# Neighbourhood attention scores: plain float32 matmuls on 64x64 tiles of the array in place of split operands on the whole array

## The chip, the core and the metric

The kernel runs on one core of a Trainium2 chip. A core has five engines with a queue each, which work side by side and wait for one another through semaphores: PE (TensorE, matrix multiplication; PEld is its weight load), DVE (VectorE), ACT (ScalarE), POOL (GpSimd) and SP (SyncE, which here issues nearly all DMA transfers). PE reads SBUF and writes PSUM, which has eight banks of 128 partitions x 2 KB. The metric is the device time of one execution in microseconds.

## The reference

One layer of a bidirectional encoder over 1024 tokens of width 1024, all in float32: a token mixer, a cross-attention into 256 memory tokens and a gated feed-forward part, each with a residual and a layer norm. The mixer has a recurrent group (mLSTM) and a neighbourhood-attention group of 8 heads x 64, whose outputs go side by side through one output projection. Only the second group matters here. The 1024 tokens are a grid of 16 rows x 64 columns, and each query sees a window of 8 rows x 16 columns, clipped at the borders, with a learned bias by relative place:

```python
s = jnp.einsum('bhrqd,bhrkd->bhrqk', qg, k_rows) * (NA_DIM ** -0.5)
...
s = jnp.where(mask, s + bias, -jnp.inf)
p = jax.nn.softmax(s, axis=-1)
o = jnp.einsum('bhrqk,bhrkd->bhrqd', p, v_rows)
```

## The kernel before

The program runs as a chain of stages. The stage of this change stands between the recurrent group and the output projection of the mixer. `nqk_d` in DRAM holds the transposed queries and keys, `nv_d` the values; an earlier stage wrote them.

**Blocks.** The stage loops over four pairs of heads `p` and four column blocks `cb`. A block is 16 of the 64 grid columns; the keys that it can see lie in 32 columns from `CB[cb]` on. Its 16 grid rows are four groups `g` of 4 rows x 16 columns, 64 queries; groups 0 and 3 see 8 rows of keys (256 keys of the 32 columns), groups 1 and 2 see 12 rows (384). Partitions 0 to 63 of a query or key tile belong to the first head of the pair, 64 to 127 to the second.

**One group.** A score tile `S` in PSUM has the 64 queries of the first head in its partitions 0 to 63, those of the second in 64 to 127, and the keys along the free dimension. `mm3` (L223 to L226) makes it with three matmuls over the whole 128x128 array: each operand is split into a rounded part (`h`) and a remainder (`l`) in the type float32r, and the products h·h, h·l and l·h are summed. So that one matmul serves both heads, the query tile is block-diagonal: 64x64 of one head, 64x64 of the other, zeros elsewhere, set once by memsets (L1131, L1132). ACT makes `qsh` (L1189, two copies per block) and `kh` (L1193), POOL the remainders `qsl` (L1190) and `kl` (L1194), in the first block DVE. Then DVE adds the bias table `tb` and takes the minimum (L1209, shown as a custom operation), ACT takes the exponential and its sum (L1211), DVE inverts and scales (L1213, L1214), PE transposes in pieces of 128 keys (L1219, into `tp`), ACT copies to `PT` (L1220). The value matmuls `o` (L1145, `pv_gen`) of a block follow during the next block: plain float32, one per head and piece, each on 64 columns of the array, so that the two heads use its two column halves. ACT and DVE split the result into `X2h` and `X2l` (L229, L230).

**Tables.** `tb` is mask minus bias, three tables per column type (groups 1 and 2 share one), built by POOL (L1181) from `wide`, one DMA per pair. There are three column types, and column blocks 1 and 2 share one.

**Work beside it.** `out_a` is the first half of the output projection, over the recurrent group's output: `fill` matmuls (L224 to L226, 128x512, twelve per half of a 128-token tile) into the one bank of tag Z. DVE adds the residual (L1089), which frees the bank; POOL adds the bias `bmo` (L1094); SP stores the tile to `part` (L1096) and loads the next residual `r` from `h` (L1072). The second half, `out`, over this stage's output, follows and partly overlaps the last pair. `mix` (L30) interleaves `na_gen` with `out_a` by the costs that they yield.

**Order.** The tile framework puts each engine's instructions into one fixed order, which a timeline model of its own sets at build time; each engine then works strictly in that order. Tags and buffer counts say which tiles share memory: a score bank comes from tag Y (three banks), the value bank from X (two). A load into memory that an earlier stage used waits for that stage. Tiles of the pool `vecs` (`vec0` to `vec2`) exist through the whole program, those of `nw` only from this stage on. In the same stretch the framework has also placed small work of the next stage: the load of the cross-attention bias `b_xo` into `vec2` (L114) and its scaling on DVE (L1453).

## Time and profile before

| | us |
|---|---|
| three timed runs, median (lowest to highest) | 1490.12 (1489.53 to 1491.66) |
| the profiled execution | 1489.96 |
| its span, first to last instruction | 1488.2 |
| PE busy over the span | 1434.5 (96%) |
| DVE, ACT, POOL busy | 1032.6, 823.8, 574.8 |
| first score matmul of the stage | 478.2 |
| last value matmul of the stage | 620.2 |

Durations of matmuls are modelled to the end of a pipeline in which the next one already runs; how long one occupies PE is read from the distance between starts. A plain float32 matmul leaves two records, one for each of its two passes. The granted clock is PE's share of its full speed.

### The profile page before, as it was taken

To read this page: it belongs to the slowest core of one execution; us is meant where nothing else is said; L and a number is where in the kernel's file an instruction comes from. 1 tells how busy PE (TensorE), PEld (TensorE's weight loads), DVE (VectorE), ACT (ScalarE), POOL (GpSimd) and SP (SyncE) were. 2 spreads that over 40 slices of the span, in tenths; PEclk is the share of its full clock that TensorE was granted. 3 is DMA by queue.
4 is the path that set the end of the run, shared out by engine and by line. 5 is a ranking of instruction groups with operands and counts; after the bars stand their busy time and mean duration, and the time that the engine had idled before them with its cause. 6 is when DMAs were issued, how large, how long until landed. Compare 5 with 4: busy or idle time off the path is not lost. (4 is left out here: it accounts for less than half of the span.)

```text
span 1488.2 us, 21528 instructions
## 1 busy us (share of the span) xinstructions
PE 1434.5 (96%) x7996; PEld 843.5 (57%) x7996; DVE 1032.6 (69%) x1945; ACT 823.8 (55%) x1393; POOL 574.8 (39%) x453
## 2 busy tenths in 40 slices
PE   8999899999999899899999799999999999999998
PEld 6998776456666677674444344444444444444444
DVE  7867866546677678588654968887788789707424
ACT  5766465564554577424545767777777766503000
POOL 4452356403324677055112444443444310300543
PEclk9999999999999999999999899999999999999999
DMA  8846653225654553643423233233233336703121
GB/s 304 317 174 204 191 192 142 76 49 144 159 144 154 188 167 131 250 134 70 92 64 114 94 121 128 114 127 116 116 136 117 133 129 238 262 29 106 51 71 57
DMA packets 116383, 208.61 MB, mean 140 GB/s; under 512 B 40627, under 2 KB 69555, under 8 KB 112950
## 3 DMA queue, kind: packets, MB, share of 16 engines
q1 hardware_dynamic: 115984, 206.47, 41.6%
q8 instruction: 63, 1.03, 0.3%
q0 software_dynamic: 144, 0.49, 0.2%
q14 instruction: 42, 0.34, 0.1%
q10 hardware_dynamic: 150, 0.27, 0.0%
HBM read 154.15 MB, written 45.15 MB: 134 GB/s over the span
## 5 line engine op out<-in xcount | busy, mean ns | idle before, releaser
L1543 POOL TENSOR_TENSOR wraw<-ur 128x512 f32<-128x512 f32 x22 | 45.5, 2068 | 205.8 <-issue 190.5
L225 PE MATMUL dn<-wlo,yp 128*128 128x512 f16 (+1 forms) x284 | 105.1, 370 | 0.0
L224 PE MATMUL dn<-whi,yp 128*128 128x512 f16 (+1 forms) x284 | 104.9, 370 | 0.0
L226 PE MATMUL dn<-whi,yp 128*128 128x512 f16 (+1 forms) x284 | 104.4, 370 | 0.0
L1631 DVE SCALAR_TENSOR_TENSOR cbuf<-C,wdw,cbuf 128x1024 f32<-128x1024 f32 x44 | 70.6, 1604 | 35.6 <-ACT cbuf L1630 35.4
L226 PEld LDWEIGHTS <-wlo 128*128 128x128 f16 x540 | 52.8, 98 | 57.2 <-DVE wlo L204 1.9
L225 PEld LDWEIGHTS <-whi 128*128 128x128 f16 x540 | 52.8, 98 | 54.6 <-issue 1.7
L224 PEld LDWEIGHTS <-whi 128*128 128x128 f16 x540 | 52.8, 98 | 53.2 <-ACT whi L203 0.3
L242 POOL TENSOR_TENSOR lnrs<-lnrs,mhalf 128x1 f32<-128x1 f32 x32 | 24.9, 778 | 133.7 <-DVE lnrs L241 94.7
L204 DVE SCALAR_TENSOR_TENSOR wlo<-wraw,us,whi 128x1024 f16<-128x1024 f32 (+1 forms) x48 | 62.5, 1320 | 19.6 <-ACT whi L203 19.6
L1632 DVE SCALAR_TENSOR_TENSOR cbuf<-C,wdw,cbuf 128x1024 f32<-128x1024 f32 x44 | 70.6, 1603 | 0.7
L252 ACT ACTIVATE r<-r,lnrs 128x1024 f32<-128x1024 f32 x19 | 23.5, 1238 | 80.5 <-DVE lnrs L251 66.4
L203 ACT ACTIVATE whi<-wraw,us 128x1024 f16<-128x1024 f32 (+1 forms) x48 | 51.1, 1102 | 15.8 <-DVE us L176 15.7
L1630 ACT ACTIVATE cbuf<-C,bdw,wdw 128x1024 f32<-128x1024 f32 x44 | 54.2, 1235 | 8.4 <-DVE C L1668 7.8
L225 PEld LDWEIGHTS <-yp 128*128 128x128 f16 x370 | 36.2, 98 | 39.9
L224 PEld LDWEIGHTS <-yp 128*128 128x128 f16 x370 | 36.2, 98 | 39.8
L226 PEld LDWEIGHTS <-yp 128*128 128x128 f16 x370 | 36.2, 98 | 39.7
L224 PE MATMUL tk<-whi,Bo 128*128 128x256 f16 (+1 forms) x192 | 52.5, 274 | 2.3 <-DVE stage L204 2.3
L225 PE MATMUL tk<-wlo,Be 128*128 128x256 f16 (+1 forms) x192 | 52.4, 274 | 0.8 <-DVE wlo L204 0.8
L224 PE MATMUL tk<-whi,Be 128*128 128x256 f16 (+1 forms) x192 | 52.6, 274 | 0.5 <-DVE stage L204 0.5
L226 PE MATMUL tk<-whi,Be 128*128 128x256 f16 (+1 forms) x192 | 52.5, 274 | 0.0
L226 PE MATMUL tk<-whi,Bo 128*128 128x256 f16 (+1 forms) x192 | 52.5, 274 | 0.0
(526 smaller groups left out, 4837.0 us busy)
## 6 DMA issues: line engine op xcount, KB each, us to landing
ur<-in_w_up_dram SPq DMA_DIRECT2D x22, 1024.0 KB
sv<-in_w_down_dram SPq DMA_DIRECT2D x22, 512.0 KB
y<-cbuf SPq DMA_DIRECT2D x22, 512.0 KB
ur<-y SPq DMA_DIRECT2D x11, 1024.0 KB
wraw<-in_w_down_dram SPq DMA_DIRECT2D x22, 512.0 KB
r<-h SPq DMA_DIRECT2D x11, 512.0 KB
wraw<-in_w_tok_dram SPq DMA_DIRECT2D x10, 512.0 KB
wr<-in_w_xk_dram SPq DMA_DIRECT2D x8, 512.0 KB
```

The lines of the kernel that those rows point to most:

```text
L203: A.activation(hi, src, AF.Copy, scale=s)
L204: return V.scalar_tensor_tensor(lo, src, s, hi, op0=OP.mult, op1=OP.subtract)
L224: T.matmul(ps, lh, rh, start=first, stop=False, skip_group_check=skip)
L225: T.matmul(ps, lh, rl, start=False, stop=False, skip_group_check=skip)
L226: return T.matmul(ps, ll, rh, start=False, stop=last, skip_group_check=skip)
L242: G.tensor_tensor(rs[:, 0:1], rs[:, 0:1], mhalf[:, 0:1], OP.pow)
L252: A.activation(r, r, AF.Identity, scale=rs[:, 0:1], bias=rs[:, 1:2])
L1543: G.tensor_tensor(S1, A21, A22, OP.add)
L1630: A.activation(c, C[:, 1:SEQ + 1], AF.Identity, scale=wdw[:, 1, j:j + 1], bias=bdw[:, j:j + 1])
L1631: V.scalar_tensor_tensor(c, C[:, 0:SEQ], wdw[:, 0, j:j + 1], c, op0=OP.mult, op1=OP.add)
L1632: V.scalar_tensor_tensor(c, C[:, 2:SEQ + 2], wdw[:, 2, j:j + 1], c, op0=OP.mult, op1=OP.add)
```

## The change

Scores become plain float32 matmuls without a split. Each has 64 rows (one head's 64 dimensions) and 64 columns (one group's 64 queries): one matmul per head and group. The first head lies in the upper row half of the array, the second in the lower one. For groups 0 and 1 the first head writes partitions 0 to 63 of the score bank and the second 64 to 127, for groups 2 and 3 the other way round, so that the four matmuls of a pair of groups, (0, 3) or (1, 2), address the four 64x64 tiles of the array. Both banks of a pair are asked for together, and every fourth score bank comes from tag X.

What goes with it: the query and key splits, the zeroed query tiles, and their tiles. ACT reorders a pair's queries once (`qp`, L1173), so that the queries of a block and group lie in a row. Since groups 2 and 3 hold their heads swapped, they need tables of their own: four per column type (L1182), from a second copy of the bias with swapped halves (two more DMAs per pair), and the copy to `PT` swaps the halves back. `wide` of pairs 0 and 2 lies in `nw` instead of `vec1`, and the first pair's keys lie in `vec1` instead of a weight buffer.

```diff
-    ... S="Y", ...
+    ... S="YYYX", ...
...
-            for (a_, b_), e_ in zip(qs, (V, G, G)):
-                e_.memset(a_.bitcast(F32), 0.0)
-                e_.memset(b_.bitcast(F32), 0.0)
+            GK = ((0, 8), (0, 12), (4, 12), (8, 8))
...
+            def scores(banks, pair, q, k, cb):
+
+                for g, ps in zip(pair, banks):
+                    r0, R = GK[g]
+                    for h in range(2):
+                        hs, ho = (slice(i * 64, i * 64 + 64) for i in (h, h ^ (g // 2)))
+                        anchor[0] = T.matmul(ps[ho, :R * 32], q[hs, cb, g], k[hs, r0:r0 + R, CB[cb]:CB[cb] + 32],
+                                             start=True, stop=True, skip_group_check=True)
...
-                    S.dma_start(wide, I["na_wide"][p])
+                        wide = nw.tile([128, 2, 576], F32, name="wide0", tag="wide0")
+                    S.dma_start(wide[:, 0], I["na_wide"][p].rearrange("p r c -> p (r c)"))
+                    for h in range(2):
+                        S.dma_start(wide[64 - h * 64:128 - h * 64, 1],
+                                    I["na_wide"][p, h * 64:h * 64 + 64].rearrange("p r c -> p (r c)"))
...
+                    A.activation(qp.rearrange("p (b r c) -> p r b c", b=4, c=16),
+                                 qr.rearrange("p (r b c) -> p r b c", b=4, c=16), AF.Copy)
...
-                            for rt, R, dk0 in ((0, 8, 4), (1, 12, 0), (3, 8, 0)):
+                            for g, R, dk0 in ((0, 8, 4), (1, 12, 0), (2, 12, 0), (3, 8, 0)):
+                                G.tensor_tensor(tabs[ct, g], mo_[ct, R], wides[g // 2][:, dk0:dk0 + R, x0:x0 + 32],
+                                                OP.subtract)
-                            A.activation(oh, src, AF.Copy)
-                            (V if n < 2 else G).tensor_tensor(ol, src, oh.bitcast(F32), OP.subtract)
-                        A.activation(kh, kr[:, :, k0:k0 + 32], AF.Copy)
-                        (V if n < 2 else G).tensor_tensor(kl, kr[:, :, k0:k0 + 32], kh.bitcast(F32), OP.subtract)
...
-                            ps = bank("S")[:, :nk]
-                            mm3(ps, qh[:, g, :], ql[:, g, :], kh[:, r0:r0 + R, :].rearrange("p r c -> p (r c)"),
-                                kl[:, r0:r0 + R, :].rearrange("p r c -> p (r c)"), True, True)
+                        for pair in ((0, 3), (1, 2)):
+                            banks = [bank("S") for g in pair]
+                            scores(banks, pair, q, k, cb)
+                            for g, ps in zip(pair, banks):
...
-                            A.activation(PT[:, GSLOT[g]:GSLOT[g] + 2 * nb - 1:2], pt[:, :nb, :], AF.Copy)
+                                if g // 2:
+                                    (pr, bs, hs_, qs_) = dst.ap
+                                    dst = bass.AP(tensor=dst.tensor, offset=dst.offset + 64,
+                                                  ap=[pr, bs, [-hs_[0], 2], qs_])
+                                A.activation(dst, pt[:, :nb, :].rearrange("p b (h q) -> p b h q", h=2), AF.Copy)
```

The order of the instructions changes only within this stage. Three places follow; L1150 is the new score matmul, L1207 the transpose, L1134 the value matmul, L1198 the minimum, L1202 and L1203 the inversion and scaling, L1446 the scaling of `b_xo`.

PE, some twelve score, transpose and value rows of the second pair of heads, between two runs of `fill` matmuls; before:

```order
L224 MATMUL S<-kh,qsh_5442 128x256
L1219 MATMUL tp<-ident,P 128x128 x3
L225 MATMUL S<-kl,qsh_5442 128x256
L226 MATMUL S<-kh,qsl_5443 128x256
L224 MATMUL S<-kh,qsh_5431 128x256
L224 MATMUL S<-kh,qsh_5431 128x384
L1219 MATMUL tp<-ident,P 128x128 x2
L1145 MATMUL o<-PT,vt 64x2x64 x2
L225 MATMUL S<-kl,qsh_5431 128x256
L226 MATMUL S<-kh,qsl_5432 128x256
L225 MATMUL S<-kl,qsh_5431 128x384
```

and with the change:

```order
L1150 MATMUL S<-kr,qp 64x384 x2
L1207 MATMUL tp<-ident,P 128x128 x5
L1134 MATMUL o<-PT,vt 64x2x64 x2
L1150 MATMUL S<-kr,qp 64x384 x2
L1207 MATMUL tp<-ident,P 128x128 x2
L1134 MATMUL o<-PT,vt 64x3x64 x4
L1134 MATMUL o<-PT,vt 64x2x64 x2
L1207 MATMUL tp<-ident,P 128x128 x3
L1150 MATMUL S<-kr,qp 64x256 x4
```

Three split matmuls per group become two plain ones; the pair of 256-key groups stays together as four, the pair of 384-key groups is two and two, with other work between.

SP, from the loads of the bias `bmo` and the residual on; before (the first pair's bias, keys and queries were loaded some thirty rows earlier):

```order
L1242 DMA bmo<-in_b_mix_out_dram 128x1024
L1072 DMA r<-h_72 128x1024 x2
L1197 DMA vt<-nv 128x1x128 x12
L1164 DMA wide<-in_na_wide_dram 128x576
L1172 DMA qr<-nqk 128x1024
L1173 DMA kr<-nqk 128x1024
L1164 DMA vec_6345<-in_na_wide_dram 128x576
L1172 DMA qr<-nqk 128x1024
L1173 DMA kr<-nqk 128x1024
L1096 DMA part_73<-wraw 128x1024
L114 DMA vec_7190<-in_b_xo_dram 128x1024
```

and with the change, right behind the same loads of `bmo` and the two `r`:

```order
L1160 DMA wide_5511<-in_na_wide_dram 128x576
L1162 DMA wide_5511<-in_na_wide_dram 64x576 x2
L1186 DMA vt<-nv 128x1x128 x6
L1096 DMA part_73<-wraw 128x1024
L1186 DMA vt<-nv 128x1x128 x6
L1160 DMA wide<-in_na_wide_dram 128x576
L1162 DMA wide<-in_na_wide_dram 64x576 x2
L1170 DMA qr<-nqk 128x1024
L1171 DMA kr<-nqk 128x1024
L1170 DMA qr<-nqk 128x1024
L1171 DMA kr<-nqk 128x1024
L114 DMA vec_7016<-in_b_xo_dram 128x1024
```

The first pair's bias (`wide_5511`) is now loaded here, right behind the residuals; the first store of `part` stands ahead of the second half of the values. On POOL the bias add of the first token tile (L1094) now stands ahead of all the first pair's tables instead of behind them, and the first table of group 3 is the eighth of them.

DVE, the rows around the scaling of `b_xo`; before:

```order
L1213 RECIPROCAL mn<-mn 128x1
L1453 TENSOR_SCALAR vec_7190<-vec_7190 128x1024
L1214 TENSOR_SCALAR P<-P,mn 128x256
L1213 RECIPROCAL mn<-mn 128x1
L230 TENSOR_TENSOR X2l<-o,X2h 64x16x16
L1214 TENSOR_SCALAR P<-P,mn 128x384
L1089 SCALAR_TENSOR_TENSOR r<-r,fill 128x512
```

and with the change:

```order
L1203 TENSOR_SCALAR P<-P,mn 128x256
L1202 RECIPROCAL mn<-mn 128x1
L1203 TENSOR_SCALAR P<-P,mn 128x384
L1089 SCALAR_TENSOR_TENSOR r<-r,fill 128x512
L1446 TENSOR_SCALAR vec_7016<-vec_7016 128x1024
L1198 ISA P,mn<-S,tb_2_5434 128x384
```

The residual add that frees the `fill` bank stood five rows behind the scaling of `b_xo` and now stands just ahead of it; the next one stands 18 rows behind.

87 lines of the change are left out of this document (33 added, 54 removed).

## Prediction

> **What bounds the kernel now.** The program before and behind this stage is the same row for row, so I read the stage alone. First the page's line of engine totals, then the busy time per stretch from the first score matmul (478 us) to the last value matmul (621 us). The columns are the stretch, its length, busy us of PE, its weight loads, DVE, ACT and POOL, then the granted clock and the DMA share.
>
> ```profile
> PE 1434.5 (96%) x7996; PEld 843.5 (57%) x7996; DVE 1032.6 (69%) x1945; ACT 823.8 (55%) x1393; POOL 574.8 (39%) x453
> 478.00:500.00 22.00, 21.21 (x118) 16.94 (x117) 15.96 (x43) 11.06 (x33) 18.12 (x20) 1.00 0.71 235
> 500.00:510.00 10.00, 5.23 (x22) 3.93 (x21) 5.61 (x14) 3.86 (x12) 5.98 (x6) 0.83 0.45 146
> 510.00:580.00 70.00, 69.28 (x450) 53.40 (x450) 55.04 (x171) 50.48 (x150) 51.97 (x55) 1.00 0.40 132
> 580.00:600.00 20.00, 16.93 (x99) 11.92 (x97) 16.47 (x47) 16.03 (x43) 11.20 (x9) 0.91 0.66 217
> 600.00:621.00 21.00, 19.42 (x134) 14.14 (x133) 12.87 (x43) 11.74 (x34) 1.98 (x1) 1.00 0.49 185
> ```
>
> From 510 to 580 us PE stands still for 0.7 of 70 us, and DVE, ACT and POOL have 15 to 20 us of slack: there PE's own work sets the pace, and work taken from the other engines buys nothing. PE loses time at two places: from 500 to 510 us, where it idles 4.8 us and the clock of 0.83 costs 10 x 0.17 = 1.7 us more (6.5 together), and from 580 to 600 us (3.1 idle and 1.8 of clock). So three questions decide: does PE's work per block grow or shrink, what becomes of the 6.5 us, and what does the changed start cost?
>
> **PE's work.** The PE timeline in the steady stretch; start, duration, line, tile, shape, records. Durations overlap, so I use the distance from one start to the next.
>
> ```profile
> 510.54 0.38 PE L1219 MATMUL tp<-ident,P 128*128 128x128 f32 x2
> 510.85 0.55 PE L1145 MATMUL o<-PT,vt 128*64 128x192 f32 x4
> 511.32 0.62 PE L224 MATMUL S<-kh,qsh 128*128 128x384 f32 x2
> 511.77 0.28 PE L225 MATMUL S<-kl,qsh 128*128 128x256 f32 x1
> 511.89 0.28 PE L226 MATMUL S<-kh,qsl 128*128 128x256 f32 x1
> 512.01 0.34 PE L225 MATMUL S<-kl,qsh 128*128 128x384 f32 x1
> 512.18 0.34 PE L226 MATMUL S<-kh,qsl 128*128 128x384 f32 x1
> 512.36 0.34 PE L225 MATMUL S<-kl,qsh 128*128 128x384 f32 x1
> 512.54 0.49 PE L1219 MATMUL tp<-ident,P 128*128 128x128 f32 x3
> 512.96 0.77 PE L1145 MATMUL o<-PT,vt 128*64 128x192 f32 x8
> 513.65 0.44 PE L226 MATMUL S<-kh,qsl 128*128 128x384 f32 x1
> ```
>
> What goes: 96 split score matmuls of 256 columns at 0.12 us (511.77 to 511.89) and 96 of 384 at 0.175 (512.01 to 512.36, two): 11.5 + 16.8 = 28.3 us.
>
> What comes: 128 plain float32 matmuls on 64 rows and 64 columns. This form is not in the trace. The nearest are plain float32 on the whole array and the value matmul on half of it:
>
> ```profile
> 383.71 0.39 PE L1006 MATMUL num<-V,whi 128*128 128x129 f32 x2
> 383.93 0.27 PE L1047 MATMUL tp<-ident,hm 128*128 128x128 f32 x1
> L1145 PEld LDWEIGHTS o<-PT,vt 128*64 128x64 f32 x256 | 14.5, 136 | 9.1 <-issue 7.8 <-ACT PT L1220 0.2 <-DVE P L1214 0.2
> ```
>
> One plain matmul leaves two records; two records of 129 columns take 0.22 us, 0.853 ns per column and pass, so 256 columns take 0.437 us and 384 take 0.655. Do tiles run side by side? At 510.85 four records of 192 columns (two heads, two passes) take 0.47 us. One after another they would need 4 x 0.164 = 0.65, side by side 0.33: the two column halves overlap, and 0.14 is left over. How the changed order groups the scores decides the rest. Its PE rows have 12 groups of four and 8 of two at 256 columns, 2 of four and 28 of two at 384: the pair of 12-row groups is nearly always torn apart by the wait for a bank. A group costs one matmul: 20 x 0.437 + 30 x 0.655 = 28.4 us, against 28.3 removed. Full packing would give 17.4, so most of the packing is not collected. The bounds: nothing overlaps, 64 x 0.437 + 64 x 0.655 = 69.9 us, and 28.4 with overlap within each group. I take 28.4, since the value matmuls are the nearest row.
>
> The array's form is now changed more often. A transpose costs 0.11 (0.42 for three, 0.31 for two), which leaves 0.09 before the switch; the value group keeps 0.14 over; the two score matmuls behind it take 0.45 instead of 0.35, 0.10 over. So a run in a narrow form costs 0.14 extra, and a return to the full form 0.09 + 0.10 = 0.19. Before: 46 narrow runs and 46 returns, 15.2 us. After, counted in its rows: 69 narrow runs (35 of scores, 34 of values) and 54 returns, 9.7 + 10.3 = 20.0. **PE's work: +0.1 + 4.8 = +4.9 us**, with nothing to hide it from 510 to 580. Below, narrow-to-narrow switches at nothing, 15 of them, would take off 2 us; above stands the dearer-entry rival.
>
> The Trainium skill's page "TensorEngine Tiling (Array Packing)", section "Restrictions and Gotchas", says that different row tiles cannot access the same PSUM bank simultaneously. Here the two heads of a group come from the two row halves and write one bank, in different partitions; no row of this trace has row tiles. By that rule the scores would cost up to the 69.9 us above, which is the first rival.
>
> **The other engines.** Rows for the whole stage, with busy us and mean ns:
>
> ```profile
> L1190 POOL TENSOR_TENSOR qsl<-qr,qsh 64x256 fp32r<-64x256 f32 x24 | 18.0, 750 | 5.4 <-ACT qsh L1189 2.6 <-PE tp L1219 1.8
> L1194 POOL TENSOR_TENSOR kl<-kr,kh 128x512 fp32r<-128x512 f32 x12 | 16.2, 1351 | 2.7 <-ACT kh L1193 2.3
> L1181 POOL TENSOR_TENSOR tb<-vec,wide 128x256 f32<-128x256 bf16 (+1 forms) x18 | 13.7, 775 | 7.0 <-DMA wide<-in_na_wide_dram 3.3 <-DVE mn L1209 3.3
> L1214 DVE TENSOR_SCALAR P<-P,mn 128x256 f32<-128x256 f32 (+1 forms) x64 | 40.9, 642 | 1.5
> L1189 ACT ACTIVATE qsh<-qr 64x256 fp32r<-64x256 f32 x24 | 9.9, 412 | 7.3 <-DMA qr<-nqk 3.9 <-PE S L225 3.1
> L1193 ACT ACTIVATE kh<-kr 128x512 fp32r<-128x512 f32 x12 | 7.5, 628 | 0.2
> ```
>
> POOL loses 30 query remainders at 0.75 and 15 key remainders at 1.35 (43 us) and gains 12 more tables at about 0.8 (10 us). ACT loses 32 x 0.41 + 16 x 0.63 = 23 us and gains four reorderings of 128x1024, some 2 x 0.63 each by the 128x512 row (5 us). Both had slack under PE up to 580 us: nothing there. From 580 to 600 us PE waits on the other engines, and ACT is busy for 16 of 20 us; the row sizes give two query copies and two key copies less there, 2.1 us. I count 0.9 of it (none to 2.1).
>
> **The start and the stall.** Timeline rows of POOL, SP, DVE and PE, with the DMA load of three stretches (last two columns):
>
> ```profile
> 473.73 7.35 POOL L1181 TENSOR_TENSOR tb<-vec,vec 128x256 f32<-128x256 bf16 x9
> 485.55 2.39 POOL L1094 TENSOR_TENSOR wraw<-wraw,bmo 128x1024 f32<-128x1024 f32 x1
> 485.89 2.20 DVE L1214 TENSOR_SCALAR P<-P,mn 128x256 f32<-128x256 f32 x1
> 475.37 0.90 SPq L1072 DMA_DIRECT2D r<-h  x2
> 476.32 12.04 SPq L1197 DMA_DIRECT2D vt<-nv  x12
> 476.00:478.00 2.00, 2.00 (x10) 1.64 (x9) 1.97 (x3) 0.45 (x2) 2.00 (x2) 1.00 0.94 233
> 478.00:480.00 2.00, 2.00 (x13) 1.91 (x12) 1.46 (x5) 0.00 (x0) 2.00 (x4) 1.00 0.87 332
> 480.00:482.00 2.00, 2.00 (x11) 1.61 (x10) 1.96 (x8) 1.80 (x6) 2.00 (x3) 1.00 0.67 257
> 479.59 0.42 DVE L1209 CUSTOM_DVE_ANT_0 P<-S,tb 128x256 f32<-128x256 f32 x1 [0.48 <-PE S L226]
> 493.53 0.43 SPq L114 DMA_DIRECT2D vec<-in_b_xo_dram  x1
> 503.47 0.69 DVE L1453 TENSOR_SCALAR vec<-vec 128x1024 f32<-128x1024 f32 x1 [3.70 <-DMA vec<-in_b_xo_dram]
> 506.19 0.80 PE L224 MATMUL fill<-whi,X1h 128*128 128x512 f32 x1 [4.77 <-DVE r L1089]
> ```
>
> *Start.* Now the first pair's bias tables are built from 473.7 us on, because that bias lay in a constants tile and was loaded early. In the change it lands in the stage's own pool, and SP issues it behind the two residual loads, at about 476.3. The transfers ahead of it keep the DMAs loaded until 482, so I put it at 483; POOL's 2.4 us bias add now stands ahead of the tables and is over by then. First table 0.7 us later, first minimum on DVE at about 484 instead of 479.6; the first of the group-3 tables is POOL's eighth, near 490. Behind DVE's minimum stand the adds that free PE's single fill bank. PE has fill matmuls for part of it (12 last 2.8 us), and waits some 3.6 us in all instead of the 0.8 of today: **+2.8 us** (0 if the load lands at once, 5 if it lands 2 us later).
>
> *Stall.* Today DVE's queue stops 3.7 us for a bias vector (b_xo) that isn't needed until much later; the add that frees the fill bank stands behind it, so PE idles 4.8 us and then gets the slow clock. In the changed DVE order the next such add stands right ahead of that operation, and the one after it 18 rows behind. In SP's changed order one store of a 128x1024 float32 tile (512 KB) fewer stands close ahead of the load. DVE should wait 0 to 2 us, under PE's next 12 fill matmuls. I take the whole **-6.5 us**; if the stall only moves, 0.
>
> **Sum**, against the profiled execution's own 1489.96 us (1.76 more than its span, 0.16 below the median of the runs): 1489.96 + 4.9 + 2.8 - 6.5 - 0.9 = **1490.3 us**. Every microsecond at the stage's end should pass on: PE is busy 19.4 of 21 us there and the program behind is unchanged.
>
> **Rivals.**
> 1. *No overlap of row halves.* 69.9 - 28.4 = +41.5 us straight on PE: 1532; with three phases per group of four, about 1521. For it: nothing in the trace shows row tiles. Against: the column halves share a bank side by side in the value rows. It decides once a second head's records start behind, not beside, the first's. The page's rule cited above speaks for this rival.
> 2. *Slower: dearer entries.* A score group may have to load four tiles one after another, 2 x 0.136 more than the value group (weight-load row), at 35 entries: up to +9.5, half of it likelier: 1495 to 1500. For it: the 0.14 over already holds a load that nothing hides. Against: the two loads of a value group don't add up today. It decides from 0.09 us per entry (+3).
> 3. *Faster: the start costs nothing and the slow stretch at 580 to 600 us shrinks.* -2.8, and half of that stretch's 4.9 us instead of 0.9 (-1.6): 1486. For it: POOL has 33 us less, and DVE's scaling of P, 0.64 us on the mean, takes 2.2 at 485.89 while POOL's add from 485.55 to 487.94 runs, so each POOL burst less shortens the chain that PE waits for there. Against: the tables are POOL's as well and come later, and ACT's reordering of pair 1 waits for the same late query load (3.9 us in the row above) as the copies did.
> 4. *The stall only moves*: 1496.8 with the rest as summed. I count it with rival 2.
>
> **Chances and range.** A run of this kernel tells about 0.2%, 3 us, from no change. Likeliest, within that: 0.40, at 1490.3, own range 1487 to 1493. Rival 1: 0.12. Rivals 2 and 4 together: 0.23. Rival 3: 0.25. So faster 0.25, same 0.40, slower 0.35. The range 1484 to 1503 holds all but rival 1 and a few hundredths.
>
> **What would show it.** Score records of one group of two starting within hundredths of a microsecond of each other, with 0.65 us to the next row at 384 columns: right; 1.3: rival 1. PE busy near 70 of 70 us again in the middle, with more of it per block. The first minimum on DVE near 484; no PE idle of 4 us behind the b_xo operation, and no clock below 1 near 506. POOL's busy time in the stage falls by some 30 us without any gain in the middle. Wrong altogether: PE idle in the middle, which would mean that DVE or a score bank, not PE, sets the pace.

## The result, and the profile after

| | before | changed |
|---|---|---|
| median of the runs, us | 1490.89 (4 runs, 1489.53 to 1493.28) | 1503.05 (4 runs, 1502.94 to 1508.27) |
| profiled execution, us | 1489.96 | 1503.11 |
| ratio to before | 1 | 1.0088, 95% interval 1.0063 to 1.0114 |

The change makes the kernel slower by 0.9%. The forecast was no change, 1490.3 us; the measured time lies at the upper end of the range, 0.05 us outside it.

The engine totals of the changed kernel show less work on DVE, ACT and POOL, as forecast, and slightly more on PE:

```profile
PE 1440.1 (96%) x8060; PEld 825.5 (55%) x8060; DVE 1018.2 (68%) x1940; ACT 806.4 (54%) x1349; POOL 541.9 (36%) x416
```

Where the time went is read from busy time per stretch. The columns are the stretch, its length, busy us of PE, weight loads, DVE, ACT and POOL, the granted clock, and the DMA share with its rate. First the kernel before (its first stretch stands in the prediction), then the changed one:

```profile
500.00:525.00 25.00, 20.23 (x117) 15.59 (x116) 16.32 (x48) 13.41 (x40) 17.47 (x18) 0.93 0.44 148
525.00:575.00 50.00, 49.28 (x322) 38.09 (x322) 40.16 (x123) 36.87 (x111) 37.45 (x39) 1.00 0.43 137
575.00:640.00 65.00, 59.29 (x346) 44.41 (x345) 45.08 (x133) 33.47 (x88) 18.33 (x14) 0.97 0.58 212
```

```profile
478.00:500.00 22.00, 18.18 (x93) 11.91 (x91) 9.73 (x28) 3.28 (x11) 15.85 (x17) 0.92 0.72 215
500.00:525.00 25.00, 21.22 (x132) 12.14 (x131) 14.59 (x49) 13.63 (x39) 10.84 (x11) 0.93 0.68 211
525.00:575.00 50.00, 48.39 (x334) 29.25 (x333) 33.48 (x111) 27.87 (x87) 20.41 (x21) 1.00 0.40 122
575.00:640.00 65.00, 56.59 (x358) 35.99 (x359) 36.81 (x129) 34.26 (x96) 14.63 (x12) 0.97 0.46 158
640.00:690.00 50.00, 47.68 (x214) 31.66 (x213) 42.12 (x71) 12.49 (x15) 24.54 (x15) 1.00 0.56 180
```

In the middle (525 to 575 us) PE is nearly as busy as before, although ACT's busy time fell by 9 us and POOL's by 17. At the start PE loses 3 us and some clock. From 500 to 525 the clock is 0.93 both times and PE idles almost as long: the stall of the old kernel has a successor. At the tail PE loses 2.7 us more, and the loss reaches past 640 us. (The same window doesn't hold quite the same work in both kernels; the sum of the table below doesn't depend on that.)

To keep the pieces apart I split PE's time from the first `fill` matmul (about 471 us) to the last `out` matmul into idle time (the PE timeline's gaps), half of each stretch in which the granted clock is 0.5, and the rest, which is work. The stretches are those of the views above.

| us | before: idle, clock | changed: idle, clock | difference | forecast |
|---|---|---|---|---|
| start, 478 to 500 | 0.8, 0 | 3.8, 1.7 | +4.7 | +2.8 |
| stall, 500 to 525 | 4.8, 1.7 | 3.8, 1.7 | -1.0 | -6.5 |
| middle, 525 to 575 | 0.7, 0 | 1.6, 0 | +0.9 | 0 |
| tail, 575 to 690 | 5.7, 1.7 | 10.7, 1.7 | +5.0 | -0.9 |
| PE work in all | 170.2 | 173.7 | +3.5 | +4.9 |
| sum | 186.4 | 199.6 | +13.1 | +0.3 |

The sums hold another 0.8 us of idle time ahead of 478 us in both. The two spans differ by 13.2 us, so the table holds all of it. Two terms were near (work and middle), three were wrong: the start by 1.9 us, the stall by 5.5, the tail by 5.9. The parts carry an error: where PE also idles inside a half-clock stretch, half of that idle time is counted twice (0.5 us idle in the changed kernel, 0.2 in the one before).

How far one execution's ledger can be trusted shows in three of the kernels further down (the layer norm's bound late, the weights early, and both). Up to about 532 us they issue the same instructions in the same order as the changed kernel on every engine. Yet:

| us | changed | bound late | weights early | both |
|---|---|---|---|---|
| start, 478 to 500: idle, clock | 3.8, 1.7 | 3.0, 3.4 | 5.0, 0 | 4.3, 0 |
| 500 to 525: idle, clock | 3.8, 1.7 | 4.7, 0 | 5.2, 1.7 | 3.0, 3.4 |
| both | 11.0 | 11.1 | 11.9 | 10.7 |
| ACT's wait for the second pair's queries | 6.60 | 5.26 | 7.41 | 7.98 |

So the sum of the two stretches holds to about 1 us, a single stretch only to about 1 us of idle time and one or two steps of 1.7 us of clock. Ahead of the stage PE, ACT and DVE have the same order in all twenty kernels here, and still the first `fill` matmul comes between 469.4 and 473.9 us; so spans differ by up to some us more or less than the ledgers.

The waits behind the idle time, from the timelines of DVE, POOL, ACT and PE of the changed kernel (start, duration, engine, line, and in brackets the idle time before it with its releaser):

```profile
483.31 9.17 POOL L1182 TENSOR_TENSOR tb<-vec,wide 128x256 f32<-128x256 bf16 x12 [1.69 <-DMA wide<-in_na_wide_dram]
484.01 0.42 DVE L1198 CUSTOM_DVE_ANT_0 P<-S,tb 128x256 f32<-128x256 f32 x1 [4.91 <-POOL tb L1182]
484.50 0.65 PE L1150 MATMUL S<-vec,qp 64*64 64x256 f32 x4 [1.94 <-DVE mn L1198]
500.29 1.06 ACT L1173 ACTIVATE qp<-qr 128x1024 f32<-128x1024 f32 x1 [6.60 <-DMA qr<-nqk]
502.15 0.63 PE L1207 MATMUL tp<-ident,P 128*128 128x128 f32 x3 [1.99 <-ACT PT L1213]
516.72 0.69 DVE L1089 SCALAR_TENSOR_TENSOR r<-r,fill 128x512 f32<-128x512 f32 x1 [3.99 <-DMA r<-h]
517.47 0.50 PE L224 MATMUL fill<-whi,X1h 128*128 128x512 f32 x1 [1.79 <-DVE r L1089]
603.89 1.06 ACT L126 ACTIVATE whi<-wraw 128x1024 fp32r<-128x1024 f32 x1 [2.76 <-DMA wraw<-in_w_mix_out_dram]
605.18 1.22 DVE L196 TENSOR_REDUCE sc<-vec 128x1 f32<-128x1024 f32 x1 [3.10 <-DMA vec<-in_ln_w_dram]
606.13 0.44 PE L1134 MATMUL o<-PT,vt 128*64 128x128 f32 x4 [3.02 <-ACT PT L1213]
607.86 0.90 PE L1207 MATMUL tp<-ident,P 128*128 128x128 f32 x4 [1.29 <-DVE sc L174]
```

All have one form: an instruction near the head of a strictly ordered queue waits for a transfer, and something that PE needs stands behind it. At 500.29 it is ACT's new reordering of the second pair's queries, one instruction for a whole pair; the copies to `PT` stand behind it. At 516.72 it is the residual add that frees the `fill` bank. At 603.89 and 605.18 it is work of the next stage, a weight split on ACT and a bound over the layer norm's weights on DVE.

The score matmuls themselves did what the prediction hoped. PE timeline of the changed kernel, in the middle:

```profile
550.94 0.86 PE L1150 MATMUL S<-kr,qp 64*64 64x384 f32 x4
551.73 0.44 PE L1207 MATMUL tp<-ident,P 128*128 128x128 f32 x2
```

```profile
553.60 1.29 PE L1150 MATMUL S<-kr,qp 64*64 64x256 f32 x12
554.83 0.77 PE L1207 MATMUL tp<-ident,P 128*128 128x128 f32 x5
```

Four records (two heads, two passes) of 384 columns take 551.73 - 550.94 = 0.79 us, which is the 0.655 of one matmul and the 0.14 of entry. The twelve at 553.60, four matmuls of 256 columns and two of 384, take 1.23 us: 0.437 + 0.655 + 0.14. The rows merge the trace's single records; these show the overlap directly. The two heads of the first group start at 550.940 and 550.946 us, the four matmuls of the 256-column pair at 553.601, 553.608, 553.615 and 553.621.

### The profile page after: what moved, and what is told of

The parts are those of the page before. It is cut to its first block, busy times and chain, and to the rows that moved or that the text cites. A ratio compares the mean times of both kernels' runs of the same rounds, so it can differ in the third digit from the quotient of the medians.

```text
span 1501.4 us, 21532 instructions
## 1 busy us (share of the span) xinstructions
PE 1440.1 (96%) x8060; PEld 825.5 (55%) x8060; DVE 1018.2 (68%) x1940; ACT 806.4 (54%) x1349; POOL 541.9 (36%) x416
```

## The experiments

Theory A, formed from the rows above: the array works as forecast, and the time went into waits for transfers that the strict queues now reach too early, or that come later. Its rivals: row tiles overlap only in part (the prediction's first), or the engines' chain around the scores is now the bound, so that PE's share is beside the point. In the ledgers below, idle, clock and work are meant as in the table, for the profiled execution, which can lie several us from the median; ratios are to the kernel before, timed beside it.

### Do four tiles overlap, and is packing worth having?

**Only two tiles at a time.** The first head always writes the lower partitions, so groups of a pair no longer address four different tiles. The swapped bias, its tables and the swap back go.

```diff
-    hs, ho = (slice(i * 64, i * 64 + 64) for i in (h, h ^ (g // 2)))
+    hs, ho = (slice(i * 64, i * 64 + 64) for i in (h, h))
-    for g, R, dk0 in ((0, 8, 4), (1, 12, 0), (2, 12, 0), (3, 8, 0)):
+    for g, R, dk0 in ((0, 8, 4), (1, 12, 0), (3, 8, 0)):
```

> The changed kernel without the swapped heads of groups 2 and 3 (and so without swapped bias copies and tables of their own): only two of the four array tiles are used at a time. If four matmuls really run side by side in the changed kernel: 64 groups one after another, 32 x 0.437 + 32 x 0.655 = 34.9 us of scores instead of 28.4, +6.5 us, less 1 to 2 us for the lighter start: about 1508. If the four-tile packing brings nothing: 1501 to 1502.

Measured: 1504.99 us, ratio 1.0098 (1.0077 to 1.0119). Work rose from 173.7 to 180.2 us, by 6.5; idle fell from 20.7 to 16.7. By the fixed stretches nearly all of that lies between 500 and 525 us, but in this kernel the gap behind ACT's reordering merely comes earlier (3.86 us at 496.6, just ahead of 500). What is gone is the start: without the two further bias loads and the fourth table PE idles 0.6 us from 478 to 496 us instead of 3.8 up to 500. The same piece of the PE timeline as above, in this kernel:

```profile
551.81 1.73 PE L1151 MATMUL S<-kr,qp 64*64 64x256 f32 x12
553.47 0.77 PE L1205 MATMUL tp<-ident,P 128*128 128x128 f32 x5
```

1.66 us instead of 1.23: the difference of 0.43 is one more group of 256 columns. So the four tiles do overlap in full, and the swap is worth 6.5 us of PE's work. It also brings the start's idle time, some 3 us, so about 2 us are left of it in the median.

**Full packing.** The four score matmuls of a pair of groups go out together, the second group first, so the 384-column pair is no longer torn apart; 22 runs of scores instead of 35.

```diff
-    for g, ps in zip(pair, banks):
+    lead = None
+    for g, ps in list(zip(pair, banks))[::-1]:
...
+            with tc.issue_after(lead.ins) if lead is not None else nullcontext():
...
+            lead = lead or anchor[0]
```

> The changed kernel, with the two score matmuls of the first group of a pair put behind the first of the second group on PE, so that four stay together: 22 runs of score matmuls instead of 35, 16 pairs of 384 keys by four instead of 2. If PE's work decides: 14 x 0.655 us less for scores and 13 runs less at 0.14 to 0.33, -11 to -13 us, about 1491. If the wait for the second bank makes the scores late for the other engines: 1497 to 1503.

Measured: 1508.85 us, ratio 1.0140 (1.0113 to 1.0166), slower than the change itself. In the profiled execution, the slowest of the four at 1514.19 us, work fell by 12.8 us, to 160.9, but idle rose by 12.6 and the clock's loss by 12.0. (Here 2.8 us of idle time lie inside half-clock stretches; without counting them twice, work falls by 11.6 and the clock's loss rises by 10.8.) PE timeline and stretches of this kernel:

```profile
541.29 1.31 PE L1152 MATMUL S<-kr,qp 64*64 64x384 f32 x16
542.53 0.50 PE L224 MATMUL fill<-whi,X1h 128*128 128x512 f32 x1
```

```profile
525.00:575.00 50.00, 43.15 (x301) 27.34 (x300) 32.73 (x112) 27.83 (x85) 19.57 (x20) 0.91 0.40 128
575.00:640.00 65.00, 52.33 (x340) 32.69 (x337) 37.84 (x130) 34.55 (x97) 15.97 (x12) 0.86 0.38 124
```

The scores of a whole block, two pairs of groups or eight matmuls, take 1.24 us: 0.437 + 0.655 + 0.14. But PE then runs out of work: the minima, exponentials and transposes of a pair come one after another, and with the scores in one lump DVE and ACT wait longer in all. PE's transposes wait 16.5 us for ACT and DVE from 478 to 640 us, against 5.0 in the change. The other engines' waits in the same stretch (what waits for what: us in all, times, longest), of the changed kernel and of this one:

```profile
ACT P L1200 <- DVE mn L1198: 15.8, 6, 10.6
DVE P L1198 <- PE S L1150: 13.9, 9, 4.2
```

```profile
ACT P L1203 <- DVE mn L1201: 33.9, 14, 10.5
DVE P L1201 <- PE S L1152: 19.5, 10, 3.2
```

By these rows the chain around PE is the bound here, and most gaps of about 2 us take the clock with them. Work taken from PE in this order brought nothing; that answers the second rival for the packed order, not for the change, whose middle stretch idles 1.6 of 50 us.

### The stall between 500 and 525 us

**The kernel before, with only the scaling of `b_xo` moved** behind this stage on DVE. This is the prediction's -6.5 us by itself.

```diff
-    V.tensor_scalar(bxo, bxo, 1.0 / ALPHA, None, op0=OP.mult)
+    with tc.issue_after(endna[0].ins):
+        V.tensor_scalar(bxo, bxo, 1.0 / ALPHA, None, op0=OP.mult)
```

> The kernel before, with only the scaling of b_xo put behind the last split of X2 on DVE. If the 6.5 us that the prediction took off for this stall were a price by themselves: 1490.9 - 6.5 = about 1484.4. If another late load takes its place as in the changed kernel: 1488 to 1491.

Measured: 1490.95 us, ratio 0.9997 (0.9981 to 1.0012): nothing. PE and DVE timelines:

```profile
503.17 0.50 PE L225 MATMUL fill<-whi,X1h 128*128 128x512 f32 x1 [1.72 <-DVE r L1090]
512.30 0.69 DVE L1090 SCALAR_TENSOR_TENSOR r<-r,fill 128x512 f32<-128x512 f32 x1 [5.55 <-DMA r<-h]
513.04 0.79 PE L225 MATMUL fill<-whi,X1h 128*128 128x512 f32 x1 [3.16 <-DVE r L1090]
```

The wait for `b_xo` is gone, and DVE gets to its next add sooner, where it waits 5.55 us for the residual `r`. PE idles 4.88 us from 500 to 525 us instead of 4.77. So the 6.5 us were never the price of `b_xo`: it was the first of two late transfers, and the second one set the end.

**The kernel before, with the transfers thinned.** The loads of the third and fourth pair's bias, queries and keys, and of `b_xo`, are issued later, `b_xo` behind the stage's last value load. By their shapes these are 3.2 MB in all; 1.9 MB of them (the third pair's loads and `b_xo`) went out ahead of 505 us in the kernel before, the fourth pair's only from 525 us on.

```diff
+    with tc.issue_after(behind[p - 1, 0].ins) if p > 1 else nullcontext():
         S.dma_start(wide, I["na_wide"][p])
...
+    with tc.issue_after(vlast[0].ins):
         bxo = vec(2, "b_xo")
```

> The kernel before, with the same loads issued later. Theory D: the residual load that followed the b_xo stall lands sooner, the 4.77 us of idle time and 1.7 us of half clock near 502 go for the most part: about 1485. Theory W2: 1489 to 1492, as with the scaling of b_xo alone.

Measured: 1485.54 us, ratio 0.9963 (0.9949 to 0.9976): the only version that is faster than the kernel before by more than the measurement is uncertain, and the fastest of all here. The residual's load (SP timeline) in the kernel before, then in this one, and what PE still waits for here:

```profile
507.97 0.33 SPq L1072 DMA_DIRECT2D r<-h  x1
```

```profile
502.46 0.33 SPq L1073 DMA_DIRECT2D r<-h  x1
503.04 0.49 PE L225 MATMUL fill<-whi,X1h 128*128 128x512 f32 x1 [1.72 <-DVE r L1090]
```

With the load 5.5 us sooner, idle from 500 to 525 us falls from 4.8 to 1.7, and no half-clock stretch is left in the stage (before: two): 3.0 + 3.4 us less, and the span is 5.1 shorter. The run with `b_xo`'s scaling moved has the same order as this one on ACT and POOL throughout the stage, on PE up to 614 us and on DVE up to 557 us; what differs ahead of that is SP's order, and the median differs by 5.4 us. So the stall was a matter of transfers, and its price was to be had without touching the scores.

**The same thinning in the changed kernel:**

```diff
+    with tc.issue_after(behind[p - 1, 0].ins) if p > 1 else nullcontext():
         S.dma_start(wide[:, 0], I["na_wide"][p].rearrange("p r c -> p (r c)"))
...
+    with tc.issue_after(vlast[0].ins):
         bxo = vec(2, "b_xo")
```

> The changed kernel, with the loads of bias, queries and keys of pairs 2 and 3 issued behind the value loads of the first block of the pair ahead, and the load of b_xo behind the stage's last value load: some 2.6 MB less in the DMA queues between 490 and 505 us. Theory D (the waits between 478 and 520 us, whichever engine shows them, are for transfers that share full DMA engines): the query load of pair 1 lands 2 to 3 us sooner, the idle time at 500 (1.99) and 516 us (1.79) and the half clock (1.71) go: about 1497.5. Theory W2 (each stall is a matter of the order of the queues and comes back elsewhere): 1501 to 1505.

Measured: 1512.17 us (the profiled execution 1517.17), ratio 1.0150 (1.0127 to 1.0174): worse by 9 than the change. ACT and PE timelines:

```profile
503.55 1.06 ACT L1176 ACTIVATE qp<-qr 128x1024 f32<-128x1024 f32 x1 [8.44 <-DMA qr<-nqk]
505.42 0.90 PE L1211 MATMUL tp<-ident,P 128*128 128x128 f32 x3 [4.12 <-ACT PT L1217]
573.42 1.06 ACT L1176 ACTIVATE qp<-qr 128x1024 f32<-128x1024 f32 x1 [7.14 <-DMA qr<-nqk]
575.05 0.69 PE L1211 MATMUL tp<-ident,P 128*128 128x128 f32 x2 [5.67 <-ACT PT L1217]
```

What helps the one kernel hurts the other: the whole-pair reordering stands early in ACT's queue, so ACT waits at it for whatever load it needs, at 573.42 for one that was made later.

**The reordering taken from ACT** (to POOL, for all pairs but the first):

```diff
-    A.activation(qp.rearrange("p (b r c) -> p r b c", b=4, c=16),
-                 qr.rearrange("p (r b c) -> p r b c", b=4, c=16), AF.Copy)
...
+    if p == 0:
+        A.activation(dst, src, AF.Copy)
+    else:
+        G.tensor_copy(dst, src)
```

> The changed kernel, with the query reordering of pairs 1 to 3 on POOL instead of ACT, so that ACT's queue no longer stops 6.6 us for the query load of pair 1. Theory W: PE's 1.99 us of idle time at 500 us and the 1.7 us of half clock behind it go, 1503.05 - 3.7 = about 1499.3. Theory P: 1501.5 to 1504. If POOL's queue stops at the same load instead and the next add of bmo is late, the residual add is late too and the gain is under 1 us.

Measured: 1502.43 us, ratio 1.0086 (1.0068 to 1.0104), 0.6 below the change and within the intervals. The stretch from 500 to 525 idles 2.4 instead of 3.8 us and keeps its clock, but the tail loses 1.7 us more at half clock and past 640 us as much again. Alone, taking the wait from ACT brings nothing measurable either.

**Both:** the thinned loads and the reordering on POOL.

```diff
+    with tc.issue_after(behind[p - 1, 0].ins) if p > 1 else nullcontext():
...
+        G.tensor_copy(dst, src)
```

> The later loads of e5 and the reordering on POOL of e2 together. Theory Q (what cost e5 its time is ACT's reordering of a pair's queries, which stands in ACT's queue ahead of the running blocks and stops it until the load lands): the gain that the later loads gave the kernel before, 5.2 us, appears, from 1502.4 to about 1497. If the late loads hurt this kernel by themselves: 1508 to 1512, as e5.

Measured: 1501.87 us, ratio 1.0084 (1.0063 to 1.0105). Now the stall is gone, as the stretch shows, and the next row shows where it went:

```profile
500.00:525.00 25.00, 25.00 (x169) 15.48 (x168) 15.98 (x55) 13.77 (x42) 15.10 (x15) 1.00 0.61 194
575.00:640.00 65.00, 53.81 (x340) 33.84 (x331) 33.49 (x121) 30.71 (x85) 11.32 (x8) 0.95 0.51 177
```

5.5 us are won from 500 to 525; from 575 to 640 PE is busy for 2.8 us less than in the change, at a lower clock. The whole kernel gains 1.2 us.

**A third buffer for the residual `r`,** so that its load needn't wait for a store.

```diff
-    for n_, b_ in (("qr", 2), ("kr", 2), ("qp", 2), ("r", 2)):
+    for n_, b_ in (("qr", 2), ("kr", 2), ("qp", 2), ("r", 3)):
...
-                        "fill", bias=bmo, rbufs=2, early=True)
+                        "fill", bias=bmo, rbufs=3, early=True)
```

> The changed kernel with three residual buffers instead of two, so that a residual load need not wait until the tile two ahead is stored. If the buffer is what makes the residual late at 516 us: the idle time of 1.79 us goes, 1501. If it is the full DMA engines: no change, 1502.5 to 1503.5.

Measured: 1506.53 us, ratio 1.0105 (1.0086 to 1.0124). PE's gap at 517 is gone, and ACT waits longer:

```profile
504.00 1.06 ACT L1173 ACTIVATE qp<-qr 128x1024 f32<-128x1024 f32 x1 [10.23 <-DMA qr<-nqk]
```

10.23 us instead of 6.60 (5.26 to 7.98 with unchanged order), with 4.94 us of idle PE behind it. In SP's order one residual load more now stands ahead of the second half of the values and of these queries, at 483.10; their own load goes out at 496.60 instead of 493.17, of which 0.9 us is the later start of the whole stage. So a load made earlier went ahead of the one that was needed first.

### The start

**The first pair's bias early:** its three transfers are issued ahead of `bmo` and the residuals.

```diff
+    wide_first = wide_of(0)
     S.dma_start(bmo, ...)
```

> The changed kernel, with the first pair's three bias loads issued ahead of the bmo and residual loads. Theory W (the loss is waits for loads that stand late): the first minimum on DVE comes near 479 instead of 484.01 us, PE's idle time from 478 to 500 us falls from 3.8 to about 0.8, the half clock behind 484.5 (1.7 us) goes: 1503.05 - 4.7 = about 1498.3 us. Theory P (the loss is PE's own work, the waits only move): within 1.5 us of the changed kernel, 1501.5 to 1504.

Measured: 1508.02 us, ratio 1.0128 (1.0107 to 1.0149). The first minimum moves from 484.01 to 479.83, and the start's loss from 5.5 to 2.4 us (4.3 to 6.4 with unchanged order). But the next waits grow:

```profile
501.94 1.06 ACT L1174 ACTIVATE qp<-qr 128x1024 f32<-128x1024 f32 x1 [8.43 <-DMA qr<-nqk]
520.39 0.50 PE L224 MATMUL fill<-whi,X1h 128*128 128x512 f32 x1 [3.56 <-DVE r L1089]
```

The stretch from 500 to 525 loses 9.4 us instead of 5.5. The residual's load goes out at 513.78 instead of 511.16; ACT's wait of 8.43 us lies little above the 7.98 that unchanged order can give. The largest loss lies elsewhere: the tail loses 6.4 us more than in the change, 5.1 of them to the clock, in a profiled execution that is the slowest of the four (1511.46 us). Why the tail is worse is not shown. So the late bias is shown as a cause of the start's loss, and this order doesn't mend it; leaving the first pair's bias in its early place, as the kernel before has it, was not tried.

### The tail

**The layer norm's bound late** on DVE, behind this stage's last split; and, by itself, **the output weights' last loads early**, from the third pair's last block on.

```diff
-    p1, s1 = pow2(ln_bound(lw, lb)[1], 14)
+    with tc.issue_after(endna[0].ins):
+        p1, s1 = pow2(ln_bound(lw, lb)[1], 14)
```

> The changed kernel, with the reductions of the next stage's layer-norm vectors (L196, which stopped DVE for 3.10 us at 602) put behind the last split of X2 on DVE. Theory W with DVE as the cause: PE's 3.0 + 1.3 us of idle time near 604 and the half clock behind it (1.7) go, about 1497 to 1498. Rival: ACT's own stop there for a weight load (2.76 us, until 603.89) holds the copies to PT nearly as long, and only some 1 to 2 us come back, 1501 to 1502.

```diff
-    with tc.issue_after(vload[0].ins):
+    with tc.issue_after(behind[2, 3].ins):
         wB.extend(...)
```

> The changed kernel, with the four weight loads of the second half of the output projection issued in front of six value loads of the last pair instead of behind them. Theory T (the loss at the stage's end, PE idle 3.0 and 1.3 us near 606 and the half clock behind, comes from the fourth weight load: ACT, which now gets there sooner, stops for it): the stop of ACT at 603.9 goes, about 1503 - 5 = 1498. If the stage's end is set by the attention's own chain of engines: no gain, 1502 to 1505.

Measured: 1503.51 us, ratio 1.0098 (1.0073 to 1.0122), and 1507.62 us, ratio 1.0114 (1.0099 to 1.0129). With the first edit PE still waits at the same place, now for ACT's weights alone: ACT waits 3.24 us for them at 603.8, PE 3.50 us at 606.0. With the second DVE waits 4.46 us for the layer norm's vector, and PE's gap is longer:

```profile
610.07 1.22 DVE L196 TENSOR_REDUCE sc<-vec 128x1 f32<-128x1024 f32 x1 [4.46 <-DMA vec<-in_ln_w_dram]
612.21 0.79 PE L224 MATMUL out<-whi,X2h 128*128 128x512 f32 x1 [5.20 <-ACT X2h L229]
```

Two waits lie side by side there, and each covers the other. The second run's 4.6 us above the change are not all of the tail: its profiled execution (1508.35 us) had lost 2.2 us by the first `fill` matmul, where nothing was changed.

**Both edits of the tail:**

```diff
+    with tc.issue_after(endna[0].ins):
+        p1, s1 = pow2(ln_bound(lw, lb)[1], 14)
...
+    with tc.issue_after(behind[2, 3].ins):
         wB.extend(...)
```

> The changed kernel with both stops at the stage's end undone at once: the weights issued earlier (e13) and the layer-norm reductions last on DVE (e3). Each alone gave nothing, since the other engine's stop lay in the same place (ACT until 603.9, DVE until 605.2). If the two stops together are the loss: idle time behind 580 us falls from 8.2 to about 5, the half clock of 1.7 goes, 1503 - 5 = about 1498. If the stage's end is set otherwise: 1502 to 1508.

Measured: 1500.87 us, ratio 1.0072 (1.0052 to 1.0091), 2.2 below the change, whose interval (1.0063 to 1.0114) it overlaps. Idle from 575 to 690 us falls from 10.7 to 7.3 us; the gaps at 606 and 608 are gone, and one of 2.93 us at 588.8 is new, behind the weight split, for which ACT now waits 3.42 us at 587.4.

### Everything together

**Thinned loads, reordering on POOL, weights early** and, in the second of these kernels, also the **bias early**:

```diff
+    with tc.issue_after(behind[p - 1, 0].ins) if p > 1 else nullcontext():
...
+    G.tensor_copy(dst, src)
...
+    with tc.issue_after(behind[2, 3].ins):
```

> The later loads and POOL's reordering of e10 with the earlier weights of e13. Theory T with theory Q: 1501.9 - 5 to 8 (e10 also had 6.8 and 3.4 us at half clock near 603 and 640) = 1494 to 1497. Otherwise 1501 to 1503.

```diff
+    first = nw.tile([128, 2, 576], F32, name="wide0", tag="wide0")
+    S.dma_start(first[:, 0], I["na_wide"][0].rearrange("p r c -> p (r c)"))
...
```

> As e14, with the first pair's bias loaded ahead of bmo and the residuals (e1). With the start undone as well: another 3 to 4.7 us, 1490 to 1493, which leaves PE's own work (+3.5) as the difference to the kernel before with its later loads (1485.5). If the earlier bias again only makes the value loads and the store of part later, as in e1: no gain over e14 or a loss of up to 5.

Measured: 1503.36 us, ratio 1.0086 (1.0071 to 1.0101), and 1509.75 us, ratio 1.0133 (1.0117 to 1.0150). In the first DVE still waits 3.5 us for the layer norm's vector, with 4.2 us of idle PE and 6.8 us at half clock behind it. In the second the early bias, which alone cost 5.0 us, costs 6.4.

**All waits but the start's:** thinned loads, reordering on POOL and weights early as above, and the layer norm's bound and `b_xo`'s scaling late.

```diff
...
+    with tc.issue_after(endna[0].ins):
+        p1, s1 = pow2(ln_bound(lw, lb)[1], 14)
...
+    with tc.issue_after(endna[0].ins):
+        V.tensor_scalar(bxo, bxo, 1.0 / ALPHA, None, op0=OP.mult)
```

> As e17, with the later loads of pairs 2 and 3 and POOL's reordering (e10), and the scaling of b_xo last. If the stops in the middle and at the end are all that the waits cost: 1501.9 - 5 = about 1496 or lower; PE's own work (+3.5) and the start (+4.7) remain against the 1485.5 of the kernel before with its later loads, which sums to 1493.7. If not: 1501 to 1505.

Measured: 1494.19 us, ratio 1.0026 (1.0012 to 1.0041).

```profile
575.00:640.00 65.00, 58.15 (x358) 37.86 (x357) 43.53 (x137) 31.37 (x86) 12.68 (x9) 0.97 0.60 216
```

That is 8.9 us less than the change, although the edits singly gave between +9 and -1 (`b_xo`'s scaling late was not run alone on the changed kernel): idle 13.3 instead of 20.7 us, none of it from 500 to 525 us, clock 3.4 instead of 5.1. Against the thinned kernel before it is 8.7 us slower, and the ledgers differ by 9.4. The start (5.6 lost against 0.9) and the work (173.9 against 171.1) account for 7.5 of that; the tail loses 3.3 us more, and the stretch from 500 to 525 us loses 1.7 less. So with most waits taken out the change still costs its own two terms, and nothing here is a gain to set against them. Much of the 8.9 us is not the change's own loss either: the thinning alone gave the kernel before 5.3 us.

**Packing with the waits taken out:** full packing with the reordering on POOL, and with the thinned loads besides.

```diff
+            with tc.issue_after(lead.ins) if lead is not None else nullcontext():
...
+    G.tensor_copy(dst, src)
```

> Four score matmuls together (e9) and the reordering on POOL (e2). If the two gains add: 0.6 us less than e9. If e9 leaves ACT's stop on the path: 3 to 4 us less than e9.

```diff
+    with tc.issue_after(behind[p - 1, 0].ins) if p > 1 else nullcontext():
```

> Four score matmuls together, reordering on POOL, later loads: all three. By theory Q with PE's work deciding: 1497 - 12 = about 1485, as fast as the kernel before with its later loads (1485.5). If the tail (late weights) decides: 1490 to 1495.

Measured: 1512.68 us, ratio 1.0151 (1.0123 to 1.0179), and 1507.52 us (four runs from 1500.03 to 1509.02), ratio 1.0113 (1.0080 to 1.0145). Work stays near 160 us, idle near 30, and 15.4 us go to the clock. Taking two of the waits out doesn't help a packed order whose gaps come from its own chain.

**The thinned kernel before, with the weights early too:**

```diff
-    with tc.issue_after(vload[0].ins):
+    with tc.issue_after(behind[2, 3].ins):
```

> The kernel before with the later loads of e6 and the earlier weights. Theory T says that ACT does not stop for the fourth weight load there, so little is to be had: 1483 to 1486, against 1485.5 of e6.

Measured: 1490.97 us, ratio 1.0007 (0.9994 to 1.0020): the 5 us of the thinning are lost again. In the profiled execution (1494.69 us) ACT waits 2.18 us for the weights at 578, PE idles 2.41 us behind it at 580.6, and a half-clock stretch follows. The split that waits for these weights stands at 578.3 instead of 580.9 in the thinned kernel, although the stage began 3.1 us later here: with an earlier load the framework put the waiting instruction earlier too.

## Why the prediction was wrong

**PE's work, +4.9: mechanism right, size 1.4 us too high.** Measured +3.5; which of the switching prices was too high stays open. A group costs one matmul, as the rows of 0.79 and 1.23 us and the run without the swap (+6.5) show, so the first rival (no overlap of row halves, 1532 us) falls, with its milder form of 1521 us, which the prediction's own groups don't give (three phases per group of four and two per group of two would be about 1525), and so does the second (dearer entries): the 384-column pair has the entry of 0.14 that was taken from the value matmuls. The Trainium skill's page "TensorEngine Tiling (Array Packing)", section "Restrictions and Gotchas", which says that different row tiles cannot access the same PSUM bank simultaneously, does not hold for this use: the two heads write one bank from two row halves, in different partitions, in 0.79 us for both, where one after the other would be 1.3.

**The start, +2.8: right as idle time, short by the clock.** The first minimum came at 484.01, as forecast, and idle rose by 3.0. Half of the idle time, 1.94 us, was not for the `fill` bank, as the prediction had it, but for a score bank, behind the same late minimum; and unchanged order gives 3.0 to 5.0 us here, so that 2.8 and 3.0 stand so close is partly luck. The gap at 484.50 was followed by 3.41 us at half clock, 1.7 more. Whether a gap there is so followed differs between executions: with the same order it was followed by 6.83 us at half clock in one kernel (gap 1.81 us) and by none in two others (2.39 and 1.70). So this term should have been 2.8 with 1.7 more as an open half.

**The stall, -6.5: the first of two steps that failed.** The prediction priced PE's idle time and the slow clock as the price of one wait, the one that the row names, and asked only whether that wait would be passed. Moving that operation alone in the kernel before gains nothing, since the next transfer is late as well. In the change two others took its place: the reordering on ACT (6.60 us) and the residual on DVE (3.99), for -1.0 in all instead of -6.5. Of these the first was named, as a point against the faster rival, and not priced. The fourth rival, that the stall only moves (1496.8 us), was the nearest; it got too small a chance, and was counted together with another.

**The tail, -0.9: the second step that failed, +5.0.** The prediction took the price of the ACT copies that fall away off this stretch and put the loads for the next stage at nothing, without a reason. The runs show these loads later. SP, DVE and ACT of the kernel before, then SP of the changed one (its DVE and ACT rows stand above, at 605.18 and 603.89):

```profile
580.14 0.36 SPq L114 DMA_DIRECT2D vec<-in_ln_w_dram  x1
588.05 1.22 DVE L196 TENSOR_REDUCE sc<-vec 128x1 f32<-128x1024 f32 x1 [0.40 <-DMA vec<-in_ln_w_dram]
592.36 0.33 SPq L125 DMA_DIRECT2D wraw<-in_w_mix_out_dram  x1
598.36 1.05 ACT L126 ACTIVATE whi<-wraw 128x1024 fp32r<-128x1024 f32 x1
```

```profile
597.30 0.51 SPq L125 DMA_DIRECT2D wraw<-in_w_mix_out_dram  x1
597.91 0.38 SPq L114 DMA_DIRECT2D vec<-in_ln_w_dram  x1
```

The fourth weight load goes out 4.9 us later, and ACT, free for its split 2.8 us later than before (603.89 - 2.76 = 601.13), waits for it. The layer norm's vector goes out 17.8 us later: its memory is the mask's, which POOL's last table frees, and that table starts at 595.90 instead of 579.42. DVE, free 14.4 us later, waits 3.10 us instead of 0.40. What the prediction lacked is the question that it asked of `b_xo`, asked of every load near the tail. With both of these waits removed the tail's idle time falls from 10.7 to 7.3 us and the median by 2.2; so they carry a good part of the +5.0, and which part exactly is not shown.

**The middle, 0:** nearly right (+0.9). POOL's busy time fell by 33 us, and ACT's by 17, with no gain. That slack under PE buys nothing held.

**Every microsecond at the stage's end passes on:** right, the span grew by 13.2 and the ledger by 13.1.

**The third rival, a free start and a shorter tail:** fell on both points.

## What to carry to other kernels

When an idle engine's row names a late transfer, look at which other transfers in the same rush are late too before pricing its removal: the gain is the time up to the next late one, not the length of the wait. When a change moves a stage's last work, ask which loads of the next stage wait for the memory that it frees, and which strict queue stops for them; when it gathers small operations into one for a whole pair, ask what queues behind the one. Here issuing 3.2 MB of loads later, 1.9 MB of them out of the rush before 505 us, was worth 5 us in the kernel before, while new score matmuls throughout the stage cost 12. And before a gap in one execution is read as an effect, look at how much the same gap differs where nothing was changed: here by about 1 us, and by 1.7 us of clock.

## What the runs showed of the hardware

The clock's losses come in a grid. In each kernel, all half-clock stretches in and around this stage start at whole multiples of 3.41 us from one another (before: 505.99 and 587.91, 24 apart; changed: 485.41, 502.48 and 608.29, 5 and 31 apart) and last 3.41 or 6.83 us. Two neighbouring cells of that grid in the changed kernel, PE's clock in the third column from the end:

```profile
481.99:485.41 3.42, 1.22 (x7) 0.34 (x5) 0.73 (x4) 0.60 (x2) 2.10 (x3) 1.00 0.53 137
485.41:488.82 3.41, 2.88 (x7) 2.31 (x8) 1.10 (x2) 0.00 (x0) 3.41 (x6) 0.50 0.48 167
```

What counts is PE's idle time within one cell, not the length of a gap. From 450 to 690 us of the twenty kernels here, 60 cells at half clock follow one at full clock; in 58 of them PE idled at least 1.77 us of the 3.41 before (in the two others 1.38 and 1.48), and the longest idle time in a cell that was not followed by half clock is 1.87 us, of a gap of 2.44 us that was split between two cells (the kernel with three `r` buffers). So a gap of just over half a cell costs 1.7 us more if it falls into one cell, and mostly nothing more if it falls across two; where it falls depends on all that came before. The Trainium skill's page "TensorE: Matmul & The Clock Gate", section "Part 1: The HAM clock gate (the "warmup" mystery)", gives a free-running window of 3413 ns, which agrees with the grid; it says that the gate closes after at least one idle window, and here a window with 1.8 to 1.9 us idle was enough.

With full packing the stage meets eight such stretches, 34 us at half clock in all, and loses 17.1 us to the clock as the table counts it, 12.0 more than the change, against 12.8 saved in work. Denser bursts with gaps of 2 us between them were slower here than thinner steady work.
